# Convolution taps held behind the RWKV substitution, its mean and norm later, softmax division on another engine, squares summed in pairs, the first down products of a feed-forward one tile later

## The chip, the cores and the metric

The kernel runs on one core of a Trainium2 chip. The core has a matrix engine (PE, with PEld for the loading of its weights), a vector engine (DVE), an activation engine (ACT), a general engine (POOL), and DMA queues, of which this kernel uses the one that SP issues. The metric is the device time of one execution in microseconds (us); lower is better.

## The reference

Two layers of a first block and then one layer of a second block work on 256 tokens of width 1024, all in float32. What one layer of the first block computes:

```python
for l in range(DEPTH):                                   # DEPTH = 2
    x = x + 0.5 * _swiglu(_rms_norm(x, norm_ffn1[l]), ffn1_w_gate[l], ffn1_w_up[l], ffn1_w_down[l])
    h = _rms_norm(x, norm_mix[l])
    proj = (h @ w_in[l]).astype(jnp.float32)
    y_rwkv = _rwkv7_mixer(...)      # 6 heads of 64: state_t = state*w + (state @ a) b + v k, y = state @ r
    y_attn = _attention_mixer(...)  # 6 heads of 64, three dilations, softmax over 256 keys
    y_conv = _conv_mixer(...)       # 256 channels, below
    mix = jnp.concatenate([y_rwkv, y_attn, y_conv], axis=-1)
    x = x + mix @ w_out[l]
    x = x + 0.5 * _swiglu(_rms_norm(x, norm_ffn2[l]), ffn2_w_gate[l], ffn2_w_up[l], ffn2_w_down[l])

def _conv_mixer(u, dw_w, dw_b, ln_w, ln_b):
    z = u[..., :D_CONV] * jax.nn.sigmoid(u[..., D_CONV:])
    z = <causal depthwise convolution of z, CONV_WIDTH = 31 taps> + dw_b
    mu = jnp.mean(z, axis=-1, keepdims=True)
    var = jnp.mean(jnp.square(z - mu), axis=-1, keepdims=True)
    z = (z - mu) * lax.rsqrt(var + CONV_LN_EPS) * ln_w + ln_b
    return jax.nn.silu(z)
```

The feed-forward width is 2816, which is 22 tiles of 128. The second block has an attention of 8 heads with a relative bias, a short convolution, pooling, an output product, a feed-forward of the same form and two layer norms.

## The kernel before

**Products.** Each float32 product is made of three PE products of split operands (`mm3`: high by high, high by low, low by high). Weights come as raw tiles of 128 x 1024 through SP's DMA queue (tile `raw`, 3 buffers); ACT copies the high half out (`hi`, L272, 6 buffers), DVE subtracts it to get the low half (`lo`, L273, 5 buffers). Activations are split alike: ACT makes `xh`, DVE `xl`.

**Order.** In the layers PE works in the order in which the code is written. The order on DVE, ACT, POOL and SP is made by a scheduler at build time, which weighs what is ready when; each engine then works its list strictly in order.

**Feed-forward.** For each of the 22 tiles `columns` makes the gate and up products (32 x 3 matmuls), `gate` (L558) forms silu(gate) times up, `rest` (L514) splits the result into `hh` (ACT, L517) and `hl` (DVE, L519), and the down products of the tile before are issued there: the list `wait` holds one tile. The last four tiles stay in the list and are worked off block by block at the end (`ends`), each finished block of x going at once into the next norm. Tile 0's gate and up products are made at the end of the stage before.

**Norm.** For each of the eight blocks of x, `Norm.tile` makes `xh` (ACT, L405) and `xl` (DVE, L406), and `square` makes the block's square on ACT (L419) and adds it to the running sum (L421): on POOL, one add after the other, seven in a norm; in the very first norm on DVE. This happens in five places between stages, called transitions below, at about 203, 363, 567, 761 and 919 us.

**Mixers.** RWKV is worked in two chunks of 128 tokens. The inverse of a small triangular system is built by substitution on DVE (L902 and after: shuffle, multiply and add, a chain of dependent instructions on 16 x 16 blocks), then masked into `X32` (L975, L976) and transposed (L977), and PE goes on with it (`at<-X,XM`). The convolution is a chain of 30 DVE instructions for each of two halves of channels (`ca<-z,lpk,ca`, L760, 60 in a layer), closed by an ACT scaling (L761). The scheduler strews these taps over DVE's list wherever it finds room. PE then sums the channels by a product with ones (`at<-ca,ones`), DVE subtracts the mean (L1136), ACT squares (L1138, `csq`), PE sums again.

Softmax (`scores`): DVE adds the bias and takes the row minimum (L594), ACT makes the exponential with its sum (L596), DVE divides by the sum (L601). `run(n)` issues n further steps (of 3 matmuls each) of the projection by w_in, which fill the spaces between the small RWKV products.

## Time and profile before

| | |
|---|---|
| median of 3 runs | 1433.05 us (1430.57 to 1433.1) |
| the profiled execution | 1431.9 us, of which the span of the profile is 1430.1 us |
| busy: PE, DVE, ACT, POOL | 1371.2, 956.9, 773.9, 73.9 us |
| mean granted clock of PE | 0.986 of full speed |

How to read it: a time is that of a whole execution. The span runs from the first to the last instruction that the profile has, so 1.8 us lie around it. Times within the trace are us from the span's start. A granted clock of 1.0 is 2.4 GHz, one of 0.5 is 1.2 GHz. An engine's busy time does not count waiting.

### The profile page before, as it was taken

What the parts mean: (1) busy time and instruction counts of PE and PEld (TensorE: products, weight loads), DVE (VectorE), ACT (ScalarE), POOL (GpSimd) and SP (SyncE); (2) the same over time, 40 slices, a digit from 0 to 9 for tenths busy, and PEclk for the clock granted to TensorE, in tenths of its full rate; (3) what the DMA queues carried; (4) which work ended last, traced back from release to release, by engine and by line L of the source; (5) the groups of instructions that cost most, each with busy time, mean ns of one, the idle gap of its engine ahead of it and who ended that gap; (6) DMA issues with size and microseconds to landing.
All of it is one profiled execution on the core that took longest, in us unless ns stands there. A gap on an engine that the chain in (4) does not pass through costs nothing. (4 is left out here: it accounts for less than half of the span.)

```text
span 1430.1 us, 28575 instructions
## 1 busy us (share of the span) xinstructions
PE 1371.2 (96%) x11786; PEld 1335.5 (93%) x11786; DVE 956.9 (67%) x1644; ACT 773.9 (54%) x1293; POOL 73.9 (5%) x92
## 2 busy tenths in 40 slices
PE   8999999997899999999999997999999999899997
PEld 8999999987799999999999986899999979899997
DVE  6555576996665556655557897765555566777775
ACT  5444456573444445544446655554444576777764
POOL 1000011100100001100002200200000000000000
PEclk9999999998999999999999999999999999999998
DMA  7666664521566665556665341365566544466551
GB/s 221 194 188 178 182 194 136 162 91 37 161 205 183 186 180 165 175 187 181 188 197 162 104 164 38 112 188 181 179 187 183 182 143 135 143 184 187 180 180 57
DMA packets 67859, 231.66 MB, mean 162 GB/s; under 512 B 7656, under 2 KB 11408, under 8 KB 67728
## 3 DMA queue, kind: packets, MB, share of 16 engines
q1 hardware_dynamic: 67728, 229.83, 52.9%
q8 instruction: 92, 1.51, 0.4%
q14 instruction: 39, 0.32, 0.1%
HBM read 227.69 MB, written 2.11 MB: 161 GB/s over the span
## 5 line engine op out<-in xcount | busy, mean ns | idle before, releaser
L272 ACT ACTIVATE hi<-raw 128x1024 fp32r<-128x1024 f32 (+1 forms) x390 | 410.7, 1054 | 375.8 <-PE at L283 253.1
L273 DVE TENSOR_TENSOR lo<-raw,hi 128x1024 fp32r<-128x1024 f32 (+1 forms) x390 | 474.4, 1219 | 177.7 <-issue 106.5
L283 PE MATMUL at<-xl,hi 128*128 128x256 f32 x1840 | 524.6, 285 | 11.7 <-DVE xl L406 10.7
L283 PE MATMUL at<-xh,hi 128*128 128x256 f32 x1840 | 524.5, 285 | 4.2 <-ACT hi L381 1.6
L283 PE MATMUL at<-xh,lo 128*128 128x256 f32 x1840 | 522.5, 284 | 1.4 <-DVE lo L382 1.4
L283 PEld LDWEIGHTS at<-xl,hi 128*128 128x128 f32 x1840 | 354.7, 193 | 15.8 <-DVE xl L406 15.1
L283 PEld LDWEIGHTS at<-xh,hi 128*128 128x128 f32 x1840 | 355.1, 193 | 5.9 <-ACT xh L1402 1.9
L283 PEld LDWEIGHTS at<-xh,lo 128*128 128x128 f32 x1840 | 354.8, 193 | 2.1 <-DVE lo L382 2.1
L283 PE MATMUL mm<-hh,hi 128*128 128x256 f32 x880 | 247.1, 285 | 4.6 <-ACT hh L517 4.6
L283 PE MATMUL mm<-hl,hi 128*128 128x256 f32 x880 | 249.4, 284 | 0.0
L283 PE MATMUL mm<-hh,lo 128*128 128x256 f32 x880 | 249.0, 284 | 0.0
L283 PEld LDWEIGHTS mm<-hh,hi 128*128 128x128 f32 x880 | 167.8, 192 | 5.8 <-ACT hh L517 5.8
L283 PEld LDWEIGHTS mm<-hl,hi 128*128 128x128 f32 x880 | 169.7, 193 | 0.3 <-DVE hl L519 0.2
L283 PEld LDWEIGHTS mm<-hh,lo 128*128 128x128 f32 x880 | 169.7, 193 | 0.0
L283 PE MATMUL mm<-xh,hi 128*128 128x256 f32 x512 | 150.1, 293 | 0.0
L283 PE MATMUL mm<-xl,hi 128*128 128x256 f32 x512 | 145.3, 284 | 0.0
L283 PE MATMUL mm<-xh,lo 128*128 128x256 f32 x512 | 145.2, 284 | 0.0
L560 DVE TENSOR_TENSOR gu<-at,R 128x512 f32<-128x512 f32 x88 | 60.7, 691 | 123.5 <-PE at L283 122.8
L283 PEld LDWEIGHTS mm<-xh,hi 128*128 128x128 f32 x512 | 97.9, 191 | 4.6 <-issue 2.8
L283 PEld LDWEIGHTS mm<-xl,hi 128*128 128x128 f32 x512 | 98.0, 191 | 0.7 <-issue 0.3
L283 PEld LDWEIGHTS mm<-xh,lo 128*128 128x128 f32 x512 | 97.9, 191 | 0.5 <-issue 0.5
L517 ACT ACTIVATE hh<-h 128x256 fp32r<-128x256 f32 x110 | 45.5, 414 | 72.5 <-DVE h L564 68.4
(297 smaller groups left out, 1359.2 us busy)
## 6 DMA issues: line engine op xcount, KB each, us to landing
raw<-ffn SPq DMA_DIRECT2D x328, 512.0 KB, 3.6
raw<-win SPq DMA_DIRECT2D x60, 512.0 KB, 3.8
raw<-wout SPq DMA_DIRECT2D x24, 512.0 KB, 3.4
raw<-win SPq DMA_DIRECT2D x8, 384.0 KB, 3.2
bias<-dbias SPq DMA_DIRECT2D x12, 128.0 KB, 3.3
lpk<-pack SPq DMA_DIRECT2D x2, 625.0 KB, 5.2
x<-x SPq DMA_DIRECT2D x4, 256.0 KB, 7.7
raw<-ffn SPq DMA_DIRECT2D x4, 256.0 KB, 6.0
```

The source lines that it names most:

```text
L272: act.activation(hi[:, :n], raw[:, :n], AF.Copy)
L273: dve.tensor_sub(lo[:, :n], raw[:, :n], hi[:, :n].bitcast(F32))
L283: placed(pe.matmul(out, lhsT, rhs, start=start, stop=stop, skip_group_check=True))
L517: act.activation(hh, h, AF.Copy)
L560: dve.tensor_tensor(gu, b, R[:, None, :].to_broadcast([128, 2, T]), op=OP.mult)
```

## The change

Seven edits, none of which changes what is computed beyond the order of a sum:

1. `lo` gets 6 buffers in place of 5. To make room, `rba` (head norm factors) moves into the pool of tiles `u3`.
2. `behind` ties the first tap of each convolution half to come after the transpose at L977 in DVE's list, without a wait on it. As each tap depends on the one before, all 60 taps come after.
3. The product with ones over `ca`, the mean and the squares move behind chunk 0's output products; the sum of the squares and the norm factor move behind the products with `km` and `sg`; the spreading of the factor moves behind chunk 1's output products. `run(3)` and `run(5)` become `run(2)` and `run(4)`.
4. The division of softmax becomes an ACT instruction.
5. Squares: each pair is summed on DVE, and POOL adds pairs: four DVE adds and three POOL adds in a norm.
6. The first down products of a feed-forward come one tile later: `rest(1, ..., False)` leaves tile 0's in the list, and at tile 2 the loop issues those of tiles 0 and 1.
7. The loads of the attention biases are held in the order of the code on SP's queue.

```diff
-        lo = wts.tile([128, 1024], F32R, name="lo", bufs=5)
+        lo = wts.tile([128, 1024], F32R, name="lo", bufs=6)
...
+    def behind(i, first):
+
+        tc.add_manual_dep(i.ins, first.ins.name, mybir.DependencyInfo(mybir.DependencyClass.NoSync, mybir.DependencyReason.DATA),
+                          reason="behind")
...
-            if n:
-                (dve if first else pool).tensor_tensor(sq, sq, self.sq, op=OP.add)
+            if n % 2:
+                dve.tensor_tensor(sq, sq, self.sq, op=OP.add)
+                if n > 1:
+                    pool.tensor_tensor(sq, sq, self.pair, op=OP.add)
+                self.pair = sq
             self.sq = sq
...
-            def rest(i, b, wd):
+            def rest(i, b, wd, put=True):
...
-                if wait and i <= NF - self.tail:
+                while put and wait and i <= NF - self.tail:
                     for d in range(ND):
                         down(d, *wait[0])
-                    wait.pop()
+                    wait.pop(0)
...
-                rest(1, b, ws[2])
+                rest(1, b, ws[2], False)
...
-                nc.sync.dma_start(b, bias_of(h))
+                tc.keep_in_program_order(nc.sync.dma_start(b, bias_of(h)))
...
-                    dve.tensor_scalar(P[:, c0:c1], P[:, c0:c1], rc[:, j:j + 1], None, op0=OP.mult)
+                    act.activation(P[:, c0:c1], P[:, c0:c1], AF.Identity, scale=rc[:, j:j + 1])
...
-                dve.scalar_tensor_tensor(ca[j], z[:, j, k:k + T], lpar("taps", j * TAPS + k), ca[j], op0=OP.mult, op1=OP.add)
+                t = dve.scalar_tensor_tensor(ca[j], z[:, j, k:k + T], lpar("taps", j * TAPS + k), ca[j], op0=OP.mult, op1=OP.add)
+                if k == 0:
+                    behind(t, y32)
...
-            rb = tmp.tile([128, 768], F32, name="rba", bufs=2).rearrange("p (c n) -> p c n", c=2)
+            rb = u3("rba")[:, :768].rearrange("p (c n) -> p c n", c=2)
```

The order of the mixer's code, in the form of a diff with the moved blocks named in brackets by what they hold:

```
         S0 = ...                                      (the state after chunk 0)
+        [chunk_y(0), yv(1), br[1], rv: chunk 0's outputs]
+        run(2)
         [taps, ca by ones, mean, csq]
-        [chunk_y(0), yv(1), br[1], rv: chunk 0's outputs]
-        run(3)
-        [b2: csq by ones, rc = token_rsqrt]
         U = chunk_u(1)
         [Dc, gw: products with km and sg]
+        [b2: csq by ones, rc = token_rsqrt]
+        chunk_y(1, U)
+        run(4)
         [rs: spread of rc]
-        chunk_y(1, U)
         [ca scaled, yb, th, silu]
-        run(5)
```

PE's list in the mixer before, where chunk 0's state is done (`br,U` to `S,AR` are chunk 0's outputs, `ca,ones` the convolution's mean, `ones,csq` its norm):

```order
L283 MATMUL at<-Vt,BK 128x128
L283 MATMUL at<-ca,ones 128x256 x2
L288 MATMUL at<-br,U 64x128 x6
L288 MATMUL at<-kr,Vt 64x128 x6
L288 MATMUL at<-AR,Bt 128x128 x6
L288 MATMUL at<-S_4018,AR 128x64 x6
L283 MATMUL mm<-xh,hi 128x256
...
L283 MATMUL at<-ones,csq 128x1 x4
L288 MATMUL at<-Rv,Yf 128x64 x6
L283 MATMUL at<-km,wr 128x256
```

And the same place in the list of the change:

```order
L283 MATMUL at<-Vt,BK 128x128
L288 MATMUL at<-br,U 64x128 x6
L288 MATMUL at<-kr,Vt 64x128 x6
L288 MATMUL at<-AR,Bt 128x128 x6
L288 MATMUL at<-S_4018,AR 128x64 x6
L283 MATMUL mm<-xh,hi 128x256
...
L283 MATMUL at<-ca,ones 128x256 x2
L288 MATMUL at<-Rv,Yf 128x64 x6
L283 MATMUL at<-km,wr 128x256
```

The four groups of chunk 0's outputs and two steps of the projection now stand ahead of the product with ones, and the sum of `csq` has gone behind the products with `km`.

DVE's list at the same place before, from the state (`S`) to the subtraction of the mean (L1136) and chunk 0's outputs:

```order
L760 SCALAR_TENSOR_TENSOR ca<-z,lpk,ca 128x256 x3
L1127 TENSOR_TENSOR S_4018<-at,D 64x192 x2
L760 SCALAR_TENSOR_TENSOR ca<-z,lpk,ca 128x256 x11
L1136 SCALAR_TENSOR_TENSOR ca<-at,ca 128x256 x2
L1113 TENSOR_TENSOR y<-y,at 128x3x128
L873 TENSOR_TENSOR br<-at,pk 128x3x128 x2
L1146 TENSOR_TENSOR Rv<-Rv,at 128x3x64 x2
```

And in the change (its line 768 is 760 of before, 1137 is 1127, 1123 is 1113, 883 is 873, 1145 is 1146):

```order
L1137 TENSOR_TENSOR S_4018<-at,D 64x192 x2
L768 SCALAR_TENSOR_TENSOR ca<-z,lpk,ca 128x256
L1123 TENSOR_TENSOR y<-y,at 128x3x128
L768 SCALAR_TENSOR_TENSOR ca<-z,lpk,ca 128x256 x3
L883 TENSOR_TENSOR br<-at,pk 128x3x128 x2
L1145 TENSOR_TENSOR Rv<-Rv,at 128x3x64 x2
L768 SCALAR_TENSOR_TENSOR ca<-z,lpk,ca 128x256
L273 TENSOR_TENSOR lo<-raw,hi 128x1024
L768 SCALAR_TENSOR_TENSOR ca<-z,lpk,ca 128x256
L273 TENSOR_TENSOR lo<-raw,hi 128x1024
L768 SCALAR_TENSOR_TENSOR ca<-z,lpk,ca 128x256 x8
L1155 SCALAR_TENSOR_TENSOR ca<-at,ca 128x256 x2
```

Behind the state eleven taps stood before and fourteen stand now, and the output instructions and two low halves of weights have moved in among them.

DVE's list in the first transition before, from the third norm block to the last (`xl` is a norm block, `x` the residual add that ends a block, `lo` a weight):

```order
L406 SCALAR_TENSOR_TENSOR xl<-x,pk,xh 128x256
L570 SCALAR_TENSOR_TENSOR x<-mm,x 128x256 x2
L273 TENSOR_TENSOR lo<-raw,hi 128x1024
L406 SCALAR_TENSOR_TENSOR xl<-x,pk,xh 128x256 x2
L570 SCALAR_TENSOR_TENSOR x<-mm,x 128x256 x3
L406 SCALAR_TENSOR_TENSOR xl<-x,pk,xh 128x256
L273 TENSOR_TENSOR lo<-raw,hi 128x1024
L406 SCALAR_TENSOR_TENSOR xl<-x,pk,xh 128x256 x2
```

And in the change, from the second to the last (its 411 is 406, 578 is 570, `sq` is the new add of a pair):

```order
L411 SCALAR_TENSOR_TENSOR xl<-x,pk,xh 128x256
L426 TENSOR_TENSOR sq<-sq 128x256
L411 SCALAR_TENSOR_TENSOR xl<-x,pk,xh 128x256
L578 SCALAR_TENSOR_TENSOR x<-mm,x 128x256 x2
L273 TENSOR_TENSOR lo<-raw,hi 128x1024
L411 SCALAR_TENSOR_TENSOR xl<-x,pk,xh 128x256
L426 TENSOR_TENSOR sq<-sq 128x256
L411 SCALAR_TENSOR_TENSOR xl<-x,pk,xh 128x256
L578 SCALAR_TENSOR_TENSOR x<-mm,x 128x256 x3
L273 TENSOR_TENSOR lo<-raw,hi 128x1024
L411 SCALAR_TENSOR_TENSOR xl<-x,pk,xh 128x256
L426 TENSOR_TENSOR sq<-sq 128x256
```

Four adds have come into DVE's list; one low half of a weight that stood ahead of the third block is gone from here (it is made earlier), and of the two later ones that stood ahead of a block one is left.

## Rows read from the trace of the kernel before

**Rows 1.** The page's busy times: engine, busy us, share of span, instructions

```profile
PE 1371.2 (96%) x11786; PEld 1335.5 (93%) x11786; DVE 956.9 (67%) x1644; ACT 773.9 (54%) x1293; POOL 73.9 (5%) x92
```

**Rows 2.** Waits of PE: engine, line, releaser, total us, times, longest

```profile
PE at L283 <- ACT ca L761: 14.1, 2, 7.1
PE at L283 <- DVE xl L406: 10.7, 10, 1.6
PE mm L283 <- ACT hh L517: 4.6, 4, 2.1
```

**Rows 3.** Windows: us, busy (x instructions) of PE, PEld, DVE, ACT, POOL, clock, DMA

```profile
203.00:216.00 13.00, 10.68 (x83) 9.96 (x82) 11.88 (x19) 9.17 (x20) 7.88 (x7) 1.00 0.39 118
...
331.30:337.70 6.40, 6.40 (x51) 5.35 (x51) 2.15 (x5) 1.24 (x3) 0.00 (x0) 0.53 0.01 3
```

**Rows 4.** Timeline of PE, layer 0's convolution sum: start, us, instruction, idle before

```profile
323.62 0.60 PE L283 MATMUL at<-ca,ones 128*128 128x256 f32 x2
331.27 1.22 PE L283 MATMUL at<-ca,ones 128*128 128x256 f32 x2 [7.05 <-ACT ca L761]
...
338.87 0.95 PE L283 MATMUL at<-ones,csq 128*128 128x1 f32 x8
...
344.01 0.88 PE L288 MATMUL at<-br,U 128*64 128x128 f32 x12
```

**Rows 5.** Timeline of DVE, the same place

```profile
317.88 1.22 DVE L273 TENSOR_TENSOR lo<-raw,hi 128x1024 fp32r<-128x1024 f32 x1
...
321.87 1.01 DVE L873 TENSOR_TENSOR br<-at,pk 128x384 f32<-128x384 f32 x2
...
324.24 0.72 DVE L1127 TENSOR_TENSOR S<-at,D 64x192 f32<-64x192 f32 x2
324.98 5.69 DVE L760 SCALAR_TENSOR_TENSOR ca<-z,lpk,ca 128x256 f32<-128x256 f32 x11
...
334.02 0.55 DVE L1113 TENSOR_TENSOR y<-y,at 128x384 f32<-128x384 f32 x1 [0.73 <-PE at L288]
...
337.81 0.61 DVE L1146 TENSOR_TENSOR Rv<-Rv,at 128x192 f32<-128x192 f32 x2
```

**Rows 6.** Timeline of PE, the first product behind the substitution

```profile
290.43 0.73 PE L283 MATMUL at<-X,XM 32*32 32x16 f32 x68 [2.28 <-DVE X L975]
```

**Rows 7.** Source lines of the division and the exponential: min/median/max ns, times

```profile
L601 DVE TENSOR_SCALAR P<-P,rc x40: 270/299/349, 276.7 to 1177.9; 128x128 f32<-128x128 f32 x20, 128x256 f32<-128x256 f32 x20
L596 ACT ACTIVATE P<-P,mx x40: 384/448/509, 274.0 to 1176.2; 128x128 f32<-128x128 f32 x20, 128x256 f32<-128x256 f32 x20
```

**Rows 8.** Timeline of ACT and PE where the state's copies end

```profile
312.63 0.86 ACT L1078 ACTIVATE XA<-at 64x384 f32<-64x384 f32 x2
...
313.94 1.26 PE L283 MATMUL at<-Yf,XA 64*64 64x64 f32 x18
```

**Rows 9.** Timeline of the first transition, DVE and POOL

```profile
204.63 0.48 DVE L406 SCALAR_TENSOR_TENSOR xl<-x,pk,xh 128x256 fp32r<-128x256 f32 x1
...
208.84 1.81 DVE L406 SCALAR_TENSOR_TENSOR xl<-x,pk,xh 128x256 fp32r<-128x256 f32 x2
...
213.11 1.82 DVE L406 SCALAR_TENSOR_TENSOR xl<-x,pk,xh 128x256 fp32r<-128x256 f32 x2
...
208.44 1.93 POOL L421 TENSOR_TENSOR sq<-sq 128x256 f32<-128x256 f32 x2 [0.71 <-ACT sq L419]
```

**Rows 10.** Timeline of PE, the first transition

```profile
209.84 0.39 PE L283 MATMUL at<-xl,hi 128*128 128x256 f32 x1 [1.15 <-DVE xl L406]
...
214.11 0.39 PE L283 MATMUL at<-xl,hi 128*128 128x256 f32 x1 [1.04 <-DVE xl L406]
```

**Rows 11.** Timeline of PE, first down products of three feed-forwards

```profile
27.92 0.74 PE L283 MATMUL mm<-hh,hi 128*128 128x256 f32 x4 [1.39 <-ACT hh L517]
...
386.97 0.74 PE L283 MATMUL mm<-hh,hi 128*128 128x256 f32 x4 [2.10 <-ACT hh L517]
...
585.46 0.74 PE L283 MATMUL mm<-hh,hi 128*128 128x256 f32 x4 [0.72 <-ACT hh L517]
```

More of the change, by code (lines that the diff above doesn't have):

```diff
@@ L369, in __init__ @@
             self.raw = [wts.tile([128, 1024], F32, name="raw", bufs=3) for j in range(2)]
-            self.w = [(wts.tile([128, 1024], F32R, name="hi", bufs=6), wts.tile([128, 1024], F32R, name="lo", bufs=5)) for j in range(2)]
+            self.w = [(wts.tile([128, 1024], F32R, name="hi", bufs=6), wts.tile([128, 1024], F32R, name="lo", bufs=6)) for j in range(2)]
         def load(self, h):
@@ L976, in mixers @@
         dve.tensor_scalar(X32[:, :, 16:32], X16, m1, None, op0=OP.mult)
-        dve.transpose(Y32, X32)
+        y32 = dve.transpose(Y32, X32)
         run(8)
@@ L1127, in mixers @@
             dve.tensor_tensor(S0[p], b[p, :, p], D[p, :, None].to_broadcast([64, 3, 64]), op=OP.mult)
+        chunk_y(0, U)
+        yv(1)
+        br[1] = masked(1, Bt, 1, 1, "br")
+        rv = Rv[1].rearrange("p (f j i) -> p f j i", f=3, j=2)
+        b = [bank("at")[:, :192].rearrange("p (f i) -> p f i", f=3) for hh in range(2)]
+        both([(b[h % 2][:, f], AR[p, f, 1, 0], S0[p, f], f == 0) for h, f, p, hc in heads])
+        for hh in range(2):
+            dve.tensor_tensor(rv[:, :, hh], rv[:, :, hh], b[hh], op=OP.add)
+        run(2)
         for j in range(2):
@@ L1138, in mixers @@
             act.activation(csq[j], ca[j], AF.Square)
-        chunk_y(0, U)
-        yv(1)
-        br[1] = masked(1, Bt, 1, 1, "br")
-        rv = Rv[1].rearrange("p (f j i) -> p f j i", f=3, j=2)
-        b = [bank("at")[:, :192].rearrange("p (f i) -> p f i", f=3) for hh in range(2)]
-        both([(b[h % 2][:, f], AR[p, f, 1, 0], S0[p, f], f == 0) for h, f, p, hc in heads])
-        for hh in range(2):
-            dve.tensor_tensor(rv[:, :, hh], rv[:, :, hh], b[hh], op=OP.add)
-        run(3)
-        b2 = bank("at")
-        for j in range(2):
-            for c in range(2):
-                mm(b2[:, c:c + 1], csq[j][:, c * 128:c * 128 + 128], ones[:, 0:1], j == 0 and c == 0, j == 1)
-        rc = token_rsqrt(b2[:, :2], 2, 1.0 / 256, 1e-5, "nc")
         U = chunk_u(1)
@@ L1165, in mixers @@
             act.activation(gw[:, f], b[:, T:2 * T], AF.Identity, scale=lpar("rwkv_ln_w", f))
+        b2 = bank("at")
+        for j in range(2):
+            for c in range(2):
+                mm(b2[:, c:c + 1], csq[j][:, c * 128:c * 128 + 128], ones[:, 0:1], j == 0 and c == 0, j == 1)
+        rc = token_rsqrt(b2[:, :2], 2, 1.0 / 256, 1e-5, "nc")
+        chunk_y(1, U)
+        run(4)
         rs = bank("at")[:, :T]
         spread(rs, rc)
-        chunk_y(1, U)
         for j in range(2):
```

## The prediction

> **What bounds the kernel now.** I read the page's busy times first: PE works 1371.2 of a span of 1430.1 us [rows 1], so it is the bound, and only its waits, about 59 us, and stretches at the lower clock can be won. The waits of PE come next [rows 2]. Three lines matter for this change: 14.1 us in two waits for the last instruction of the convolution (one in each layer), 10.7 us in ten waits for norm blocks (the transitions, of which there are five, so 2.1 us each), and 4.6 us in four waits for the first `hh` of a feed-forward.
>
> Then the places. At the convolution PE starts two matmuls at 323.62, finds the second half's taps unfinished and goes on at 331.27, having idled 7.05 us [rows 4]. After the stall the granted clock is 0.53 on average up to 337.7 [rows 3], that is mostly 1.2 GHz; PE pays twice. DVE's rows show why it is late: eleven taps in one chain stand last, 324.98 to 330.67, 0.52 us each as every tap waits for its forerunner [rows 5]. So DVE's total of work decides there, and PE only waits. In front of that lies another wait, 2.28 us for the substitution [rows 6], also DVE's. In the first transition DVE is busy 11.88 of 13 us [rows 3] and the waits for `xl` are 1.15 and 1.04 us there [rows 10], with a smaller one between.
>
> **The change part by part.**
>
> *Squares in pairs.* DVE gains four adds in each norm and loses none (but in the first norm, where it loses three). An add is a two-input instruction of 256 columns, like the taps and `xl`: 0.42 us by the residual's form, 0.33 when the next overlaps it; I take 0.33 to 0.48 [rows 9]. So 1.3 to 1.9 us more of DVE. POOL loses four adds of 0.97 us (1.93 for two [rows 9]). What that gives DVE back: an `xl` takes 0.48 us alone, two of them beside POOL 1.81 and 1.82 [rows 9], where some 0.9 would do; 0.9 us for two, and about 2.3 us in the whole transition with a third such place, or 0.33 for each of seven adds. Four fewer give 1.3 us. By quantity the two cancel.
>
> The gain is in order. Before, the fourth `xl` stands behind a `lo` and runs beside POOL's adds; in the new list one `lo` is out of the way, and POOL's second add starts only after DVE's add of the pair. I walked the new list with these durations: the fourth `xl` ends near 208.5 in place of 209.8, so the wait of 1.15 goes. Two weight copies now stand on ACT ahead of the sixth block's `xh` (some 2 us), so the middle wait grows to about 1.3; behind it the last, 1.04, goes. Three waits of 2.6 us become one of 1.3. I take 1.2 for each of five transitions: **6.0 us**. Bounds: the whole of the 10.7 us, or, if nothing comes back from POOL, 1.3 us of loss in each, 6.6.
>
> The Trainium skill's page "SBUF — State Buffer", section "Who interferes with whom", says more: a GpSimd instruction that reads SBUF and a VectorE instruction with two SBUF inputs exclude each other for the whole instruction. Beside POOL our `xl` loses 0.45 us, not the 0.97 of a POOL add, so the trace shows half of that; if the whole were excluded, four fewer adds would free up to 3.9 us of DVE in a transition, and the waits for `xl` could go entirely (a rival below).
>
> *Taps behind the substitution.* In DVE's list 16 of a layer's 60 taps stood ahead of the transpose. They come after it now, at 0.52 us in one chain as in the last eleven [rows 5], or some 0.40 (the 0.48 of a like instruction less an overlap of 0.08, as in the pairs of [rows 9]) where two chains alternate: 6.4 to 8.3 us more of DVE between the substitution and the last tap. Against that: the chain of the substitution has fewer strangers in it (softmax's division, and part of its bias adds, also leave), about ten instructions of 0.3 to 0.5 us, so X32 comes some 3 to 5 us sooner on DVE (an estimate from the two lists), and the wait of 2.28 goes. DVE's short waits for PE in that stretch fill up with taps.
>
> *Division on ACT.* DVE's instruction takes 0.27 to 0.35 us; ACT's nearest form, the exponential on the same tile, 0.38 to 0.51 [rows 7]. Twelve in a layer: DVE 3.6 us less, ACT 5 more. ACT has room but in one place: the third pair of heads, where four of them come between the exponentials and the copies that PE waits for. Those end at 313.49, and PE starts at 313.94 [rows 8]: cover 0.45 us. Four cost 1.6 (0.3 to 0.4 each where they overlap), so PE may wait 0 to 1.2; I take 0.8. Of the 2.28 won, 1.5 remain. The 16 divisions of the second block I put at nothing, since PE has its products there to hide them; without cover one pair costs 0.9.
>
> *Convolution's mean and norm later.* What is late next is the last tap. S is now at 324.24 - 1.5 = 322.75. Behind it on DVE stand: S 0.7, `y` 0.55, `br` 1.0, `Rv` 0.6, two `lo` of 1.2, six taps of 0.40 and eight of 0.52 [rows 5], together 11.8, less overlaps of some 0.4: the last tap ends at 334.15. ACT's scaling and the start took 0.6 before (330.67 to 331.27), so PE's product with ones goes at **334.8**, 3.5 us later than before. PE comes to it sooner than it did in work done, later in time: the window from 331.3 to 337.7 holds the product with ones (1.2) and chunk 0's four groups, which so took about 5.2 us at 0.53 of the clock, 2.8 at full; with six matmuls of projection 0.8 more; 323.62 - 1.5 + 3.6 = 325.7. The stall is then 9.1 us: it is moved, not removed, and the clock falls as before. Behind it remain: ones 1.2, and the products with `Rv`, `km` and the sum of `csq`, which from 338.87 to 344.01 took 5.1 at full clock [rows 4], with 0.3 for the spread that now comes later. In the first 6.1 us after the stall, at about 0.53, PE does the 1.2 and 2.6 of the 4.8; 2.2 remain: chunk 1's outputs start at 334.8 + 6.1 + 2.2 = 343.1 against 344.01. But three matmuls (0.4) that had been done are still to do, so 0.5 us are won. In both layers: **1.0 us**. Bounds per layer: +4 if the last tap is 4 us later, when all 16 taps come on top; -7 if it is early enough that the clock holds.
>
> *First down products a tile later.* The waits were 1.39, 2.10 and 0.72 us [rows 11] (and what is left of the 4.6, 0.4, in the second block). PE goes on with tile 2's gate products in place of tile 0's down products. Those need tile 2's `hi` and `lo`. In the second layer's first feed-forward, the new list has these ahead of `gu`, and 0.72 is won. In the first feed-forward and in the first layer's second, tile 2's `lo` stands in DVE's new list behind the same `h` that `hh` waits for, and it takes 1.2 us where `hh` takes 0.4 on ACT. There I expect the wait under another name and about as long. Sum **0.7 us**, between +2 and -3.5.
>
> *`lo` buffers, bias loads, `rba`:* nothing; DVE's idle and ACT's hide a `lo` that comes sooner or later, and a bias load of 128 KB lies between raw loads. If a bias came late, its softmax would wait for one load; no PE wait for a load stands among the waits.
>
> **The sum:** 6.0 + 1.0 + 0.7 = 7.7. The profiled execution took 1431.9 (1.8 of it around the span), so **1424** us; against the median, 1433.05, that is 9 less, of which 1.1 is the distance of that execution from the median.
>
> **The rivals.** (a) *POOL shuts DVE out*: freeing it takes all 10.7 us of waits for `xl`, 4.7 more than I count: 1419. For it: the waits are all for `xl`; against: ACT's order, and a loss of 0.45 only. The rule of the Trainium skill's page named above works this way. (b) *The conv stall goes*: taps end early enough that PE's clock stays. It would give 7 us or more in each layer, 1424 - 13 = 1411. Against: fourteen taps and 4.6 us of other work stand behind S. (c) *The gains are eaten*: DVE is late at S by the 16 taps, say 2 us in each layer, and transitions give half: 1432, no change that a measurement tells; here too falls that the change does nothing because each wait turns up at the next instruction. (d) *Slower*: the pair adds are paid on DVE, and POOL's absence gives nothing back: 1.3 us of loss in each of five transitions in place of 1.2 won, 1424 + 12.5 = 1436.5. It decides where a POOL add less gives DVE under 0.33 us; the whole is slower than 1435.9 from about 1.2 us lost in each. For it: DVE is busy 11.88 of 13 us there.
>
> **How the numbers follow.** Forecast (1420 to 1429) 0.52, (a) 0.10, (b) 0.06, (c) 0.20, (d) 0.12. 1424 is the likeliest. A difference under 0.2% (2.9 us) can't be told from none: 1430.2 to 1435.9. Faster: 0.52 + 0.10 + 0.06 + a fifth of (c) = 0.72; same: the rest of (c) and a sixth of (d) = 0.18; slower 0.10. The range leaves (b) and most of (d) out: 1416 to 1434.
>
> **What would show it.** Right: no wait at `X` (L975 before); the wait for `ca` still there, in two of 8 to 10 us, PE's clock low after it, chunk 0's outputs ahead of it at full clock; one wait for `xl` or `xh` of about 1.3 in each transition; a wait for `lo` in place of that for `hh` at 386. Wrong: a `ca` wait under 6 or over 12 us, transitions with three waits as before, or a new wait of over 1 us for a softmax tile or a `raw` load.

## The result and the profile after

| | before | after |
|---|---|---|
| median, us | 1433.07 (1430.57 to 1433.13) | 1448.34 (1447.79 to 1450.02) |
| span of the profiled execution, us | 1430.1 | 1448.1 |
| mean granted clock of PE | 0.986 | 0.970 |

The ratio is 1.0113, with an interval of 1.0095 to 1.013: the change made the kernel 1.1% slower, 15 us, where 9 us less were forecast. The busy times of the page:

```profile
PE 1394.4 (96%) x11786; PEld 1353.9 (93%) x11786; DVE 960.1 (66%) x1621; ACT 776.7 (54%) x1333; POOL 62.7 (4%) x75
```

PE has the same 11786 products as in [rows 1] and is busy 23 us longer with them. So what was lost lies mostly in products at the lower clock: a clock of 0.970 over 1448 us is 43 us of full-speed work not granted, 0.986 over 1430 us is 20. The waits of PE (engine, line, releaser, total us, times, longest):

```profile
PE at L283 <- ACT ca L771: 15.7, 2, 7.9
PE at L299 <- ACT rba L935: 4.9, 3, 2.4
PE at L283 <- ACT hi L272: 3.4, 2, 2.0
PE at L299 <- POOL lr L1397: 3.4, 2, 2.2
PE at L283 <- DVE xl L411: 2.4, 6, 0.8
PE mm L283 <- ACT hh L525: 1.7, 1, 1.7
```

Against [rows 2] the convolution's two waits are a little longer. The norm blocks' waits for `xl` fell from 10.7 to 2.4 (those for `xh` rose from 0.6 to 2.1), the first `hh`'s from 4.6 to 1.7, with 3.4 for `hi` instead. The wait for the head norm's factors `rba` rose from 1.3 to 4.9. These waits do not add up to the loss. What does is the place of one and the same PE product in the two traces (start of the product, us):

| product | before | after | later by |
|---|---|---|---|
| end of the first transition | 219.47 | 218.12 | -1.4 |
| behind the head norm factors | 263.51 | 266.20 | 2.7 |
| first product with `X`, behind the substitution | 290.43 | 291.19 | 0.8 |
| state of chunk 0 | 313.38 | 319.03 | 5.7 |
| chunk 1's outputs | 344.01 | 351.74 | 7.7 |
| end of the mixer | 356.56 | 366.86 | 10.3 |
| behind the second transition | 377.63 | 384.94 | 7.3 |
| layer 1, behind the transition | 765.90 | 769.52 | 3.6 |
| layer 1, head norm factors | 819.56 | 826.62 | 7.1 |
| layer 1, behind the substitution | 846.28 | 851.85 | 5.6 |
| layer 1, state | 869.36 | 879.89 | 10.5 |
| layer 1, end of the mixer | 911.08 | 926.91 | 15.8 |
| second block, start | 930.87 | 945.02 | 14.2 |
| second block | 1264.35 | 1277.86 | 13.5 |
| near the end | 1422.28 | 1440.13 | 17.9 |

The transitions and the feed-forwards win, more than forecast: 1.4, 3.0, 3.7 and 1.6 make 9.7 us by this table, where 6.7 stood in the sum. Each mixer loses about 12 us, at three places (head norm, state, behind the convolution), and the last part some 4. The three places, one after the other.

**Head norm.** PE and POOL of the change (start, us, instruction, idle before it and what ended that):

```profile
259.66 1.83 PE L299 MATMUL at<-pk,rba 128*128 128x128 f32 x6 [2.36 <-ACT rba L935]
```

```profile
255.71 0.85 POOL L1041 MEMSET Yf<- 128x768 f32 x1 [8.74 <-DVE Kt L963]
256.52 2.43 POOL L310 TENSOR_TENSOR ny<-nv,mhalf 128x12 f32<-128x12 f32 x1
```

POOL of the kernel before:

```profile
255.28 2.26 POOL L305 TENSOR_TENSOR ny<-nv,mhalf 128x12 f32<-128x12 f32 x1 [7.16 <-ACT nv L921]
258.29 0.74 POOL L1031 MEMSET Yf<- 128x768 f32 x1 [0.75 <-DVE Kt L953]
```

`ny` is the inverse square root from which `rba` is made, and `Yf`'s memset fills a tile with zeros. Before, POOL made `ny` first. In the change the memset stands ahead and waits for DVE (`Kt`) while POOL could have begun: its input `nv` is there at 254.04, and `ny` starts at 256.52, 1.2 us later than before, and PE stands for `rba`. The granted clock goes to 0.5 behind it.

**State.** The windows (us, busy and instructions of PE, PEld, DVE, ACT, POOL, then PE's clock, DMA's share and GB/s), and PE in them:

```profile
306.20:309.90 3.70, 2.96 (x87) 2.55 (x86) 3.29 (x7) 3.59 (x8) 0.73 (x1) 0.99 0.02 4
309.90:320.00 10.10, 9.68 (x57) 8.25 (x57) 5.89 (x21) 6.86 (x22) 0.00 (x0) 0.50 0.00 0
```

```profile
307.86 1.55 PE L288 MATMUL at<-Vt,ka 128*128 128x64 f32 x12 [0.67 <-DVE xl L462]
310.32 1.64 PE L288 MATMUL at<-ka,q 64*128 64x128 f32 x6 [0.49 <-ACT Rv L1067]
```

Two short waits, and ten microseconds at 1.2 GHz from 309.8 on, as the second of them begins. Before, this stretch ran at full speed (state at 313.38), and the longer wait of 2.28 us that stood in front of it [rows 6] brought no fall. What makes these waits is not shown; the company that the fall keeps is. In layer 0 the clock from 305 to 320 is 0.60 to 0.67 in all five kernels with the full tie (the change and three variants of it, and the tie alone), and 1.00 in the other thirteen kernels here.

The wait at `X` is gone. DVE writes `X` at 289.61, against 289.97 before:

```profile
289.61 0.31 DVE L985 TENSOR_SCALAR X<-X,pk 128x192 f32<-128x192 f32 x1
```

That looks as if the shorter list had brought nothing. But the substitution was held up by the head norm: DVE stands 2.83 us at 261.10 for the product of `rba`. In the change with POOL's memset put behind `ny` (an experiment below) the head norm's products come 4.7 us sooner, `X` 4.95 us sooner than here and 5.3 sooner than before, and PE does not wait either:

```profile
284.66 0.32 DVE L989 TENSOR_SCALAR X<-X,pk 128x192 f32<-128x192 f32 x1
286.25 0.99 PE L283 MATMUL at<-X,XM 32*32 32x16 f32 x96
```

**Convolution.** PE, DVE and the windows:

```profile
333.69 0.68 PE L283 MATMUL at<-ca,ones 128*128 128x256 f32 x2
342.23 1.22 PE L283 MATMUL at<-ca,ones 128*128 128x256 f32 x2 [7.86 <-ACT ca L771]
351.74 0.88 PE L288 MATMUL at<-br,U 128*64 128x128 f32 x12
```

```profile
317.90 1.02 DVE L883 TENSOR_TENSOR kr<-at,pk 128x384 f32<-128x384 f32 x2 [3.20 <-PE at L288]
318.84 3.25 DVE L768 SCALAR_TENSOR_TENSOR ca<-z,lpk,ca 128x256 f32<-128x256 f32 x8
330.07 0.72 DVE L1137 TENSOR_TENSOR S<-at,D 64x192 f32<-64x192 f32 x2
337.51 4.12 DVE L768 SCALAR_TENSOR_TENSOR ca<-z,lpk,ca 128x256 f32<-128x256 f32 x8
```

```profile
334.40:342.20 7.80, 0.00 (x0) 0.00 (x0) 6.98 (x13) 0.51 (x1) 0.28 (x2) 0.67 0.48 137
342.20:351.00 8.80, 8.77 (x29) 7.58 (x29) 2.73 (x7) 2.11 (x5) 0.00 (x0) 0.51 0.00 0
```

The stall is where the forecast put it, behind chunk 0's outputs, and 7.9 us long instead of 9.1. But PE goes on at 342.2, not at 334.8. Nearly all of these 7.4 us (7.3) was there before the walk of the forecast began: `S` is written at 330.07, where 322.75 stood in it, and the last tap ends 11.56 us behind `S` (337.51 + 4.12), where 11.4 had been walked. `S` hangs on PE's products for the state, and those are what the lower clock made late. DVE's row at 317.90 shows the same from its side: with taps left in its list DVE stands idle for 3.20 us, because `kr`, which waits for a product of the slow PE, is ahead of them.

Where the taps' time went is in this window of DVE before and after (218 to 290 us):

```profile
218.00:290.00 72.00, 69.36 (x562) 66.39 (x561) 61.33 (x169) 45.46 (x88) 10.48 (x13) 1.00 0.49 150
```

```profile
218.00:290.00 72.00, 69.35 (x541) 66.62 (x541) 54.00 (x139) 44.57 (x86) 9.70 (x11) 0.95 0.47 148
```

The upper row is of the kernel before. DVE had 10.7 us free ahead of the substitution's end even with the 16 taps in it; now it has 18.0 (the division has left too), and the taps stand behind, in the stretch where PE waits for the last of them.

**The transitions** go as forecast in kind. The first has one wait that counts and a small one, where [rows 10] had two of over 1 us:

```profile
210.87 0.39 PE L283 MATMUL at<-xh,hi 128*128 128x256 f32 x1 [0.71 <-ACT xh L410]
211.49 0.39 PE L283 MATMUL at<-xl,hi 128*128 128x256 f32 x1 [0.23 <-DVE xl L411]
```

### The profile page after: what moved, and what is told of

Its sections match the earlier page's. It is cut to its first block, busy times and chain, and to the rows that moved or that the text cites. A ratio compares the mean times of both kernels' runs of the same rounds, so it can differ in the third digit from the quotient of the medians.

```text
span 1448.1 us, 28550 instructions
## 1 busy us (share of the span) xinstructions
PE 1394.4 (96%) x11786; PEld 1353.9 (93%) x11786; DVE 960.1 (66%) x1621; ACT 776.7 (54%) x1333; POOL 62.7 (4%) x75
## 5 line engine op out<-in xcount | busy, mean ns | idle before, releaser
L273 DVE TENSOR_TENSOR lo<-raw,hi 128x1024 fp32r<-128x1024 f32 (+1 forms) x390 | 477.0, 1225 | 254.3 <-ACT hi L272 253.0
L283 PE MATMUL mm<-xh,hi 128*128 128x256 f32 x512 | 154.9, 303 | 0.0
L283 PE MATMUL mm<-xl,hi 128*128 128x256 f32 x512 | 149.1, 291 | 0.0
L283 PE MATMUL mm<-xh,lo 128*128 128x256 f32 x512 | 148.9, 291 | 0.0
L283 PEld LDWEIGHTS mm<-xh,hi 128*128 128x128 f32 x512 | 102.4, 200 | 5.4 <-issue 3.4
L283 PEld LDWEIGHTS mm<-xl,hi 128*128 128x128 f32 x512 | 102.3, 200 | 0.9 <-issue 0.5
L283 PEld LDWEIGHTS mm<-xh,lo 128*128 128x128 f32 x512 | 102.1, 199 | 0.0
```

The source lines that it names most:

```text
L273: dve.tensor_sub(lo[:, :n], raw[:, :n], hi[:, :n].bitcast(F32))
L283: placed(pe.matmul(out, lhsT, rhs, start=start, stop=stop, skip_group_check=True))
```

## The experiments

The theory after this reading: two parts lose, the tie of the taps (with what it does to POOL's list and to the clock), and the sixth `lo` buffer, and the rest win about what was forecast. The rivals: that the convolution's later mean and norm lose the time, that the order of the memsets alone explains the mixers, or that the division has slowed ACT. Each experiment's ratio is against executions of the kernel before beside it, whose median lay at 1433.9 to 1434.4 us (1433.07 beside the change); so small differences between two experiments go by the ratios.

### Parts of the change undone

**Five `lo` buffers again**, and `rba` in its own tile:

```diff
-        lo = wts.tile([128, 1024], F32R, name="lo", bufs=6)
+        lo = wts.tile([128, 1024], F32R, name="lo", bufs=5)
...
-            rb = u3("rba")[:, :768].rearrange("p (c n) -> p c n", c=2)
+            rb = tmp.tile([128, 768], F32, name="rba", bufs=2).rearrange("p (c n) -> p c n", c=2)
```

> The change with 5 buffers for the low halves again (and the head norm factors in their own tile). Theory: with a sixth buffer the list of VectorE in the second block's feed-forward has the low half of the centred down weight ahead of hl, and PE waits for hl about 0.29 us in each of some 16 tiles; with 5 buffers these waits go, 4 to 5 us: about 1443.5. The waits in the mixers stay, as Yf's second fill is still ahead of the norm factor on GpSimd. Rival: the waits for hl come from the down products' order, and 5 buffers change nothing: 1448.

1435.61 us, 1.0021 times before (1.0001 to 1.0042): 12.7 us below the change, where 4 to 5 were expected. An edit that I had put at nothing is worth most of the loss. The clock from 863 to 880 is 1.00 here, 0.70 in the change. The ten executions of this kernel spread from 1430.55 us, at a mean clock of 0.984, to 1444.32, at 0.969: the same instructions, and the time goes with the clock. So the size is uncertain by some microseconds. The waits of `hl` and where they come from are shown with the buffer alone, below.

**Taps free** (the tie left out):

```diff
                 t = dve.scalar_tensor_tensor(ca[j], z[:, j, k:k + T], lpar("taps", j * TAPS + k), ca[j], op0=OP.mult, op1=OP.add)
-                if k == 0:
-                    behind(t, y32)
```

> The change without the tie of the taps to the substitution's transpose. Theory: 16 taps go back ahead of the substitution; the wait for X of some 2.3 us comes back in both layers (+4 to 5), but VectorE has 6 to 8 us less to do behind it, so that the waits for xl at 307 and the low clock after them go (-5 in each layer) and the last tap comes some 6 us sooner (part of it given away to the clock): 1434 to 1440. Rival: the low clock at 310 comes from the division on ScalarE or from the wait for the head norm's factors, and the taps do not matter: 1450 to 1453.

1427.24 us, 0.9949 (0.9934 to 0.9964): 21 us below the change. PE's first waits:

```profile
PE at L283 <- DVE X L983: 8.0, 2, 4.0
PE at L299 <- ACT rba L933: 6.2, 2, 3.2
```

The wait for `ca` is gone altogether, and that for `X` has come back as 4.0 us in each layer. So with early taps and the other edits the stall at `ca` can go; that the later mean and norm alone do not bring this, and that the division has a part in it, is shown below.

**`Yf`'s memset behind `ny`** in POOL's list:

```diff
-            pool.memset(Yf[c], 0.0)
+            behind(pool.memset(Yf[c], 0.0), ny_ins[-2 + c])
```

(`ny_ins` collects the POOL instructions that make `ny`.)

> The change with one more tie: each fill of Yf stands behind a head norm factor (ny) in GpSimd's list. Theory: PE's wait of 2.4 us for rba at 257 and 818, and the low clock that follows, come from the second fill, which waits for VectorE's Kt and holds the factor back; without it both go, 2.4 plus about 2 us in each layer: 1439 to 1441. Rival: rba is late because VectorE and the products before it are late (Kt, the transposes), and the wait only changes its name: 1446 to 1448.

1444.9 us, 1.007 (1.0049 to 1.0091): 3.4 us less than the change by the medians, some 6 by the ratios. The wait for `rba` falls from 4.9 to 1.9, but the clock still falls ahead of the state and behind the convolution (0.67 from 305 to 320, 0.72 from 328 to 352). The memset's place is a part of the loss, not its root.

**Mean and norm at the old places** (the moved blocks of code put back, `run(3)` and `run(5)`):

```diff
-        chunk_y(0, U)
-        yv(1)
...
-        run(2)
...
+        chunk_y(0, U)
+        yv(1)
...
+        run(3)
+        b2 = bank("at")
...
+        run(5)
```

> The change with the convolution's mean and norm at their old places in the code. Theory A (the later norm is worth little): the last tap comes some 4.6 us sooner, as chunk 0's outputs and two low halves no longer stand among the taps, but the four groups run at half clock after the stall; 1445 to 1449. Theory B (the later norm is what costs, through a longer stretch at half clock after the stall): 1440 to 1443. Theory C (as I forecast, it gains a little): 1449 to 1450.

1451.94 us, 1.0118 (1.0101 to 1.0135): 3.6 us more than the change by the medians, 0.7 by the ratios, and the intervals overlap. The rival falls, since nothing is won by going back. That the later norm wins the 0.5 us in a layer that had been forecast can be neither shown nor excluded here.

### Parts alone, in the kernel before

**Squares in pairs alone:**

```diff
-            if n:
-                (dve if first else pool).tensor_tensor(sq, sq, self.sq, op=OP.add)
+            if n % 2:
+                dve.tensor_tensor(sq, sq, self.sq, op=OP.add)
+                if n > 1:
+                    pool.tensor_tensor(sq, sq, self.pair, op=OP.add)
+                self.pair = sq
```

> The kernel before with the squares summed in pairs, and nothing else. My forecast's term: 1.2 us in each of five transitions, 1427 to 1429. Rival: the four adds are paid on VectorE, 1437 to 1441. Third: all waits for xl go, 1422 to 1424.

1428.32 us, 0.9956 (0.9942 to 0.9971): 6.1 us won, where the forecast's term was 6.0. PE's two longest waits, and a row of DVE that answers to [rows 9]:

```profile
PE at L283 <- ACT ca L769: 14.1, 2, 7.1
PE at L283 <- DVE xl L411: 6.8, 11, 0.8
```

```profile
209.32 0.48 DVE L411 SCALAR_TENSOR_TENSOR xl<-x,pk,xh 128x256 fp32r<-128x256 f32 x1
```

No `xl` of this transition is stretched any more (0.48 us each); [rows 9] had 1.81 us for two. Of the 10.7 us of waits 6.8 remain, so the rival in which POOL shuts DVE out and freeing it takes all of them did not come.

**The tie alone:**

```diff
+                if k == 0:
+                    behind(t, y32)
```

> The kernel before with the taps tied behind the substitution's transpose, and nothing else. Theory: the tie is what costs in the change, whatever else is there: the wait for X goes (-4 to 5 us in both layers) but the last tap comes 5 to 7 us later, the stall there grows by as much or more, and the clock falls once more ahead of it: 1444 to 1450. Rival: the tie costs only together with the other edits (the outputs and low halves among the taps, the division on ScalarE): 1430 to 1436.

1454.95 us, 1.0151 (1.013 to 1.0172): 20.5 us lost by this edit alone.

```profile
PE at L283 <- ACT ca L768: 21.8, 4, 7.6
PE at L299 <- ACT rba L932: 3.7, 3, 1.8
```

```profile
316.82 0.56 DVE L880 TENSOR_TENSOR kr<-at,pk 128x384 f32<-128x384 f32 x1 [3.16 <-PE at L288]
329.37 6.42 DVE L765 SCALAR_TENSOR_TENSOR ca<-z,lpk,ca 128x256 f32<-128x256 f32 x16
```

Here too DVE stands idle (3.16 us) with taps behind it; behind the state stand these sixteen taps in a row and six more, where eleven stood [rows 5]; and the clock is 0.66 from 305 to 320. POOL's memset has also gone ahead of `ny` here (253.57 and 254.39), without the sixth buffer: the scheduler makes all lists anew when one instruction moves.

**Half a tie**, in the kernel before, from the ninth tap of each half. The scheduler then puts 12 of a layer's taps ahead of the substitution, where 16 stood before:

```diff
+                if k == 8:
+                    behind(t, y32)
```

> The kernel before with the tie only from each half's ninth tap on: 12 taps of a layer stand ahead of the transpose in place of 16 (before) and 0 (the tie alone). Theory: what costs is the work that is moved from VectorE's free time ahead of the substitution to its full list behind it; 16 taps cost 20.5 us net of 4.8 won at X, some 25 in both layers, so 4 taps cost about 6 and win back up to 4 at X: 1435 to 1440. Rival: the tie costs by a threshold, through the low clock at 307 that comes with it; with 12 taps ahead the clock holds there and the gain at X stays: 1429 to 1433.

1434.76 us, 0.9999 (0.999 to 1.0009): neither won nor lost. The wait for `X` is nearly gone (0.36 us at 288.30), that for `ca` is 16.9 us, and the clock holds at 1.00 from 305 to 320. So four taps moved cost nothing and sixteen cost 20 us; the loss begins somewhere between, and in these two runs it comes with the fall of the clock ahead of the state.

**Mean and norm later, alone:**

```diff
+        chunk_y(0, U)
+        yv(1)
...
+        run(2)
...
-        run(3)
-        b2 = bank("at")
...
+        chunk_y(1, U)
+        run(4)
...
-        run(5)
```

> The kernel before with the convolution's mean and norm moved later, and nothing else (taps free as before). Theory A: the last tap comes some 2 us later, as chunk 0's outputs stand among the taps, PE has 4 us of work ahead of the stall, and the stall shrinks but stays: 1429 to 1433. Theory B: with free taps the stall goes whole and the low clock with it, as in the run without the tie: 1418 to 1424.

1433.08 us, 0.9992 (0.9979 to 1.0004). The wait for `ca` falls from 14.1 to 9.8 us, and the time does not move. The edit by itself is worth nothing that can be measured.

**Six `lo` buffers alone**, with `rba` in `u3`:

```diff
-        lo = wts.tile([128, 1024], F32R, name="lo", bufs=5)
+        lo = wts.tile([128, 1024], F32R, name="lo", bufs=6)
...
-            rb = tmp.tile([128, 768], F32, name="rba", bufs=2).rearrange("p (c n) -> p c n", c=2)
+            rb = u3("rba")[:, :768].rearrange("p (c n) -> p c n", c=2)
```

> The kernel before with six buffers for the low halves (and the head norm factors among the u3 tiles), and nothing else. Theory: two separate costs, the waits for hl in the second block's feed-forward (4.5 us) and Yf's second fill ahead of the head norm factor on GpSimd with a longer wait for rba and a fall of the clock (2 to 4 us in each layer): 1441 to 1447. Rival: the sixth buffer pays elsewhere (low halves in time), and it ends at 1434 to 1439.

1453.59 us, 1.0128 (1.0113 to 1.0143): 19 us lost by an edit put at nothing, and more than the 7 to 13 then expected.

```profile
PE at L283 <- DVE xl L411: 12.9, 15, 1.4
PE at L299 <- ACT rba L930: 6.1, 3, 3.0
PE mm L283 <- DVE xl L459: 2.2, 4, 0.9
```

```profile
258.16 0.85 POOL L1036 MEMSET Yf<- 128x768 f32 x1 [9.33 <-DVE Kt L958]
258.98 2.43 POOL L310 TENSOR_TENSOR ny<-nv,mhalf 128x12 f32<-128x12 f32 x1
```

The memset has gone ahead of `ny` here too, and `xl` is waited for more often. The third place is the low half `hl` of a feed-forward's product. The view of that tile says how long its readers waited (us, times), first in the kernel before, then in this one:

```profile
  PEld mm L283: 0.2, 1
```

```profile
  PEld mm L283: 5.5, 17
```

In the change it is 4.0, 15. DVE's rows in the second block show how, first at a tile of the kernel before, then at one of the change:

```profile
1269.43 0.42 DVE L1432 TENSOR_TENSOR h<-gu,s 128x256 f32<-128x256 f32 x1
1270.13 1.23 DVE L273 TENSOR_TENSOR lo<-raw,hi 128x1024 fp32r<-128x1024 f32 x1 [0.27 <-PE at L283]
1271.27 0.42 DVE L519 TENSOR_TENSOR hl<-h,hh 128x256 fp32r<-128x256 f32 x1
```

```profile
1283.91 0.43 DVE L1442 TENSOR_TENSOR h<-gu,s 128x256 f32<-128x256 f32 x1
1284.89 1.28 DVE L270 SCALAR_TENSOR_TENSOR lo<-raw,wmean,hi 128x1024 fp32r<-128x1024 f32 x1 [0.55 <-ACT hi L269]
1286.09 0.42 DVE L527 TENSOR_TENSOR hl<-h,hh 128x256 fp32r<-128x256 f32 x1
```

A `lo` stands between `h` and `hl` in both. Before it is that of L273, and the `lo` of L270 comes behind `hl` (1273.02). With a free buffer the `lo` of L270 has gone one place further ahead: it waits 0.55 us for its `hi` and takes 1.28, so `hl` comes 2.18 us behind `h` in place of 1.84, and PE's weight load waits 0.23 us at 1286.56. A tile of this feed-forward takes 8.92 us in place of 8.64. Each is small, there are some sixteen of them.

**Six buffers with the memset behind `ny`**, the edit before and

```diff
-            pool.memset(Yf[c], 0.0)
+            behind(pool.memset(Yf[c], 0.0), ny_ins[-2 + c])
```

> The kernel before with six buffers for the low halves (and the factors in u3), and Yf's fills tied behind the head norm factors. Theory: of the 19 us that the edit costs alone, the wait for rba and its low clock go, some 4 in each layer; low halves ahead of xl and hl in VectorE's list keep the rest: 1443 to 1447. Rival: the wait for rba is only one name of VectorE being late there, and it stays at 1450 to 1454.

1445.48 us, 1.0084 (1.0062 to 1.0107): 6 to 8 of the 19 us come back (6.3 by the ratios, 8.1 by the medians), and the wait for `rba` is 1.9. `xl` keeps its 12.9.

The starts of the same PE products say where the buffer's loss lies (the last norm of the kernel starts 20.9 us later than before): 6.7 us up to the two head norms, 4.2 from there to the ends of the mixers, 4.2 in the two transitions behind the mixers (8.8 lost, 4.6 given back in what follows), 5.0 in the last feed-forward. With the memset behind `ny` the first of these is 0.5.

**`rba` in `u3` alone:**

```diff
-            rb = tmp.tile([128, 768], F32, name="rba", bufs=2).rearrange("p (c n) -> p c n", c=2)
+            rb = u3("rba")[:, :768].rearrange("p (c n) -> p c n", c=2)
```

> The kernel before with the head norm factors among the u3 tiles, and nothing else. Theory: the sixth buffer is what costs, the move into u3 nothing: 1432 to 1436. Rival: the factors now wait for a u3 tile that is read late, and that holds rba: 1438 to 1445.

1432.44 us, 0.9986 (0.9975 to 0.9997). It costs nothing; the 19 us are the buffer's.

### The winning parts together

**No tie, five `lo` buffers, memset behind `ny`** (pairs, division, later norm, later down products and bias order stay):

```diff
-        lo = wts.tile([128, 1024], F32R, name="lo", bufs=6)
+        lo = wts.tile([128, 1024], F32R, name="lo", bufs=5)
...
-                if k == 0:
-                    behind(t, y32)
...
-            pool.memset(Yf[c], 0.0)
+            behind(pool.memset(Yf[c], 0.0), ny_ins[-2 + c])
```

> The change without the tie of the taps, with 5 buffers for the low halves, and with Yf's fills tied behind the head norm factors. Theory: the three costs that the earlier runs show are separate places, and add up: from 1427.2 (without the tie) the waits for hl go (4 to 5 us) and the wait for rba with its low clock (3 us or more in each layer): 1414 to 1419, faster than both kernels. Rival: PE then only comes sooner to the wait for X, which grows by what was won at rba, and only the waits for hl are won: 1422 to 1424.

1415.69 us, 0.9868 (0.9848 to 0.9887). This beats both kernels: 1.3% below before. Three of PE's waits:

```profile
PE at L283 <- DVE X L987: 8.4, 2, 4.7
PE at L283 <- DVE xl L414: 6.8, 11, 0.8
PE at L299 <- ACT rba L937: 1.9, 4, 0.8
```

There is no wait for `ca`, and the clock is 1.00 in the windows where the change's fell (305 to 320, 328 to 352, 863 to 880, 885 to 912). At the wait for `X` it does fall, to 0.89 from 285 to 300.

**The same with the division on DVE:**

```diff
-                    act.activation(P[:, c0:c1], P[:, c0:c1], AF.Identity, scale=rc[:, j:j + 1])
+                    dve.tensor_scalar(P[:, c0:c1], P[:, c0:c1], rc[:, j:j + 1], None, op0=OP.mult)
```

> The joined version (no tie, 5 buffers, fills later) with softmax's division on VectorE again. Theory: the division on ScalarE frees 3.6 us of VectorE in each layer where VectorE sets the end, so without it the wait for X or for the taps grows by 1 to 4 us in each layer: 1418 to 1424. Rival A: it is hidden, 1414 to 1417. Rival B: ScalarE's copies come sooner without the four divisions ahead of them, as my forecast priced (0.8 us in each layer): 1412 to 1414.

1422.96 us, 0.992 (0.9901 to 0.9939), 7.3 us more. With the division on DVE the `ca` wait is back:

```profile
PE at L283 <- ACT ca L772: 9.7, 2, 4.9
PE at L283 <- DVE X L987: 4.5, 2, 2.4
```

The cost that the forecast had priced is there as well: with the division on ACT, PE waits 1.9 us for the copies `XA` (0.94 in each layer), and not at all for them with the division on DVE. DVE's time is worth more.

**The same with a late tie** (from the seventh tap of each half; twelve taps stand ahead in the trace, not the nine of the expectation, and twenty without the tie):

```diff
+                if k == 6:
+                    behind(t, y32)
```

> The joined version with the tie from each half's seventh tap on: 9 taps stand ahead of the transpose, none among the last steps of the substitution. Theory: the wait for X falls from 4.7 to about 3 us in each layer, and the later taps still end in time since PE has the outputs and two steps ahead of them: 1411 to 1414. Rival: VectorE has no room behind the substitution, the wait for the taps comes back with the low clock: 1420 or more.

1421.44 us, 0.9901 (0.9886 to 0.9916), 5.7 us more than without; the rival came. The wait for `X` falls from 8.4 to 2.4 and that for `ca` rises from none to 6.6: what is taken from the one is given to the other. Both cost clock. From 285 to 300 it rises from 0.89 to 1.00, from 328 to 352 it falls from 1.00 to 0.86, and the second stretch is the longer one: 0.11 of 15 us is some 1.7 us of full speed, 0.14 of 24 us some 3.4.

**The same with the first down products at the old place:**

```diff
-                while put and wait and i <= NF - self.tail:
+                if wait and i <= NF - self.tail:
...
-                    wait.pop(0)
+                    wait.pop()
...
-                rest(1, b, ws[2], False)
+                rest(1, b, ws[2])
```

> The joined version with the first down products at their old place. My forecast's term: the later place is worth 0.7 us: 1416 to 1417. Rival: it is worth more, 2 to 4 us, as PE waits for hh and the clock falls: 1418 to 1420. Other rival: it costs, 1412 to 1415.

**And with the bias loads free:**

```diff
-                tc.keep_in_program_order(nc.sync.dma_start(b, bias_of(h)))
+                nc.sync.dma_start(b, bias_of(h))
```

> The joined version with the bias loads free again. My forecast: no difference, 1414 to 1417. Rival: the order on the queue lets the first weights land sooner and the start is 1 us or more faster with the edit: 1417 to 1419 without it.

1416.35 us (0.9878, 0.9858 to 0.9899) and 1416.05 (0.9873, 0.9855 to 0.9891): 0.7 and 0.4 more, both within the intervals. The forecast had 0.7 and nothing; the runs do not contradict it, and cannot show 0.7.

## Why the prediction was wrong

- **"`lo` buffers, bias loads, `rba`: nothing"** is the first step that failed. The reason given, idle time of DVE and ACT that hides a `lo` which comes sooner, holds for a `lo` that does not stand in anyone's way. DVE works its list in order, and PE waits for what stands behind. Alone it cost 19 us. Bias loads and `rba` were right.
- **The term of taps and convolution norm: +1.0 won.** The tie alone costs 20.5, the norm alone is worth 0. The step that failed is "S is now at 324.24 - 1.5 = 322.75": `S` came at 330.07. What was worked out on either side of it held: the walk of DVE's list behind `S` (11.4 us against 11.56), and "X32 comes some 3 to 5 us sooner", which the tie alone shows (286.18 against 289.97) and the change with the memset tied (284.66); in the change itself the late head norm ate it. Between the two lies PE's clock: I let it fall only behind the stall, as before; it fell ahead of it, at 309.8, for 10 us, and the state came 5.7 us late. "DVE's short waits for PE in that stretch fill up with taps" was wrong too: DVE stood idle 3.20 us in front of `kr` with taps queued behind. The bound that I gave for that term, +4 per layer, was too near, since it was worked out at full clock.
- **POOL's list was never walked.** The prediction follows DVE, ACT and PE, and POOL only in the transitions. The memset ahead of `ny` is in the new list of the change, and the wait for `rba` and the fall of the clock behind it follow from it: 4.1 us in layer 0 (-1.4 to 2.7) and 3.5 in layer 1 (3.6 to 7.1). Tying the memsets back wins 3.4 to 6 in the change and 6 to 8 with the six buffers alone.
- **Division on ACT** had the wrong sign. Its cost was right: 0.8 us of wait in a layer were expected, which left 1.5 of 2.28, and the joined kernel shows 0.94. But the 3.6 us that DVE saves in a layer had no price of their own behind the substitution. In the joined kernel the edit is worth 7.3 us, and with it go the `ca` wait and the lower clock behind it.
- **Right:** pairs (6.0 against 6.1 measured alone, interval 4 to 8); the stall moved behind chunk 0's outputs and not removed (9.1 against 7.9); the `hh` wait coming under another name (`hi`, 2.04 us at 394.27); bias loads and `rba`'s place. The rule of the Trainium skill's page "SBUF — State Buffer", section "Who interferes with whom", had given 1419 as a rival by exclusion for the whole instruction. With pairs alone the `xl` of the first transition are not stretched, as under the rule, but 6.8 us of the waits for `xl` stay, so something else than the stretched `xl` makes those. That it is the order of DVE's list fits the rows and was not tested. The first transition shows two waits of 0.55 and 0.80 us where one of 1.3 had been walked; that the term agrees to 0.1 us, within an interval so wide, is in part luck.

The loss can be walked in three steps: from before (1434.4 beside that run) to 1415.7 with what wins, to 1427.2 with six buffers and the memset ahead, to 1448.3 with the tie. Measured one by one in the kernel before, the parts do not add: -6.1 (pairs), +20.5 (tie), +19.2 (six buffers) and 0 (norm) make +33, where the whole is +15. Two of them share the wait for `rba`, as both put the memset ahead of `ny`, and the division gives DVE time back; how much each gives back is not settled by these runs. Nor is the rest of the buffer's 19 us: 6 to 8 go with the memset and 5.3 are waits for `hl` (5.5 less 0.2). The remaining 6 to 8 lie in the mixers behind the head norm and in the transitions behind the mixers, by the starts of the products; the longer waits for `xl` (12.9 against 10.7, and 2.2 at L459) are the nearest rows there, and no run took them away. In the joined kernel 14.1 of 18.7 us are accounted for by pairs (measured in the kernel before), division and down products (0.7, within the noise); the later norm and the memsets' order share the rest, not told apart.

No kernel ran in which the taps were placed by hand in DVE's gaps, nor one with the clock held; that the lower clock, and not the waits, makes up most of the mixers' loss is read from the windows, from PE's 23 us of longer work and from the ten executions with five buffers, whose time went with their clock.

## What to carry to other kernels

An engine's list is worked in order: before an instruction is held back, look whether the time it leaves was free and the time it goes to is full. Here 16 taps left a stretch with free time and went to one whose last instruction PE waits for. A buffer more is not free where a scheduler makes the lists: it lets something of low worth stand ahead of something that is waited for, so the new order of every engine has to be read, the nearly idle one too. A wait of PE costs more where the clock falls with it; of two places where the same wait can lie, compare what each does to the clock behind it.

## What the runs showed of the hardware

A wait's length alone did not tell whether the clock falls. At the product behind the substitution PE waited 2.37 us with the later norm alone, and the clock stayed at 1.00 from 285 to 300; in the joined kernel with the division on DVE it waited 2.41 us at the same product, and the clock was 0.50 from 289 to 293. In the change it fell to 0.50 at 309.8 and stayed there for 10 us, after a wait of 0.67 us that ended at 307.86 and as one of 0.49 us began, among products of 64 columns and, ahead of them, of 32 rows. And POOL's inverse square root of a tile of only 128 x 12 takes 2.26 to 3.15 us, some three to four times as long as its memset of 128 x 768, 0.74 to 0.85.
